# One-stream stages: high and low part of an operand side by side as one moving operand of 512 columns

## The chip, the cores and the metric

The kernel runs on one core of a Trainium2 chip. The metric is the device time of one execution in microseconds, as the median of several runs.

## The reference

Two blocks follow each other on 256 tokens `x` and 256 tokens `ctx` of width 1024, in float32. The first block has two layers, each with an FFN, a mixer (latent attention, a spatial gate and a short convolution) and a second FFN; the second block has two layers, each with a mixer (a scan with gates and a local attention) and an MLP. The modulation of every step comes from `c` and `c_ctx`. In the last layer of each block the context stream ends with the mixer's input, so that from there on only `x` goes on:

```python
def ffn_half_step(h, shift, scale, gate, g, w_in, w_out):
    a, b = jnp.split(modulate(rms_norm(h, g), shift, scale) @ w_in, 2, axis=-1)
    return h + FFN_RESIDUAL_WEIGHT * gate * ((jax.nn.silu(a) * b) @ w_out)

def sq_relu_mlp(h, w1, w2):
    return jnp.square(jax.nn.relu(h @ w1)) @ w2
...
        h = h + mod_l[5] * merge_groups(attn, sg, cv, g_out[l], w_mix_out[l])
        h = ffn_half_step(h, mod_l[6], mod_l[7], mod_l[8], g_ffn2[l], w_ffn2_in[l], w_ffn2_out[l])
        if not last:
            ...
            hc = ffn_half_step(hc, mod_c[6], mod_c[7], mod_c[8], g_ffn2[l], w_ffn2_in[l], w_ffn2_out[l])
```

The FFN is 2816 wide (its first matrix has two halves `a` and `b` of that width), the MLP 4096. The weight matrices are the bulk of the work: every product with one is done to nearly float32 precision, by the splitting told next.

## The kernel before

**Layout.** Features lie on the partitions. The residual stream is eight tiles `h` of 128 x 512 (they print as h_91 to h_98): columns 0 to 255 are `x`, 256 to 511 `ctx`. A two-stream stage works on 512 columns at once, a one-stream stage on the 256 of `x`.

**Splitting.** Every operand of a large product is the sum of a high and a low part in the type fp32r. For weights, `split_weight` has ScalarE copy the raw tile `wr` into `wh` (L316) and VectorE subtract to get `wl` (L317), in pieces of 1024 columns; a weight of 8 x 256 columns is two such pieces, called halves below. For activations, `split_from` does the same with `gh` (L612) and `gl` (L613), and the norm with `xnh` (L615) and `xnl` (L616). The class `Split` holds the parts of an operand, for one stream in two tiles of up to eight k by 256 columns.

**The products.** `mm_feat` computes one output tile of 128 features. For each of the k tiles of the contraction it issues three matmuls into one tile of PSUM: wh by the high part (L346), wh by the low part (L347), wl by the high part (L348), each with its own weight load. A PSUM tile from `psum` is 128 x 512 float32, and five of them (tag "mm") take turns; a one-stream product uses half of one.

**One-stream stages.** They are: the output projection of the last mixer of the first block (operand `ys`), the FFN after it (operands `xn` and `g`; tiles of PSUM `fa` in, `pj` out), the output projection of the last mixer of the second block, and the last MLP. The FFN goes by pairs of tiles: for each tile two products `pa` and `pb`, then `evac`: tanh of `pa` on ScalarE (L751), two VectorE operations with `pa` and `pb` (L752, L753), and the split. Its output is taken in three parts, `part_out`, the MLP's in four. In the output projections `add_residual` takes a finished tile: one VectorE operation h = h + gate x pj (L717).

**Between stages.** As residual tiles are finished, the next norm's `add` squares them and sums over the tiles (L101 on ScalarE, L103 and L106 on VectorE, tiles `acc` and `sq`). Then TensorE sums over features (`nm<-sumto`, L570), VectorE makes the reciprocal root from `ms` (L582) by a short chain on `rs` and `nt` (L584 to L590), TensorE spreads it over the partitions (L564), and the norm's tiles follow. `busy` (L553) are matmuls by the identity without a use for their result. At the very end `Final.add` scales each finished tile into `fy` (L211), and `turn` transposes it on TensorE (`fT`, L219). Within the one-stream FFN the second ctx is loaded and transposed (`xt`, L1768); at its end two tiles of the next mixer's input for ctx are computed (272 columns, L360 to L362), from which `vn` (L1297) and `gates` (L1298) are taken.

**What sets the order.** A scheduler places the instructions of each engine by its own estimate of their times; weights are loaded by SP in the order of use, with three buffers for raw and three for split weights. Within an engine the instructions then run in the order written.

Of the kernel before, what the change touches and what calls it, by code (L numbers as in the profile page):

```python
# [10 lines left out]
F32R = mybir.dt.float32r  # L11
I32 = mybir.dt.int32
AF = mybir.ActivationFunctionType
ALU = mybir.AluOpType
AX = mybir.AxisListType

P = 128
D = 1024
KT = 8
T = 512  # L20
# [22 lines left out]
class Split:  # L43


    def __init__(self, b, n, name, width=T, per=4, joint=False):
        self.b = b
        self.per = per
        self.n = n
        self.width = width  # L50
        self.name = name
        self.joint = joint
        self.parts = {}

    def part(self, which, k):
        g = k // self.per
        n = min(self.per, self.n - self.per * g)
        if (which, g) not in self.parts:
            if self.joint:
                t = self.b.arena([P, 2, n, self.width], F32R, self.name)  # L60
                self.parts["h", g], self.parts["l", g] = t[:, 0], t[:, 1]
            else:
                self.parts[which, g] = self.b.arena([P, n, self.width], F32R, f"{self.name}{which}")
        return self.parts[which, g][:, k % self.per]
# [3 lines left out]

    def L(self, k, c0, c1):
        return self.part("l", k)[:, c0:c1]  # L70


class Weight:
# [36 lines left out]
class Norm(Sumsq):  # L110


    def __init__(self, b, key, gname, gi, sh_chunk, sc_chunk, streams):
        super().__init__(b, streams)
        self.x = b.split(KT, "xn", streams)
        self.key, self.sh_chunk, self.sc_chunk = key, sh_chunk, sc_chunk
        self.gain = (gname, gi)
        self.gs = None
# [117 lines left out]
class Builder:  # L236
# [99 lines left out]
    def mm_feat(self, ps, w, m0, x, c0, c1, ks, first, last, kw0=0, m=P):  # L336
        nc = self.nc
        ks = list(ks)
        o = ps[:m, : c1 - c0]
        for i, k in enumerate(ks):  # L340
            kw = k - kw0
            st = first and i == 0
            en = last and i == len(ks) - 1
            wh = w.h[:, kw, m0 : m0 + m]
            wl = w.l[:, kw, m0 : m0 + m]
            nc.tensor.matmul(o, wh, x.H(k, c0, c1), start=st, stop=False)  # L346
            nc.tensor.matmul(o, wh, x.L(k, c0, c1), start=False, stop=False)  # L347
            self.last_mm = nc.tensor.matmul(o, wl, x.H(k, c0, c1), start=False, stop=en)  # L348
# [270 lines left out]

        return Norm(self, key, gname, gi, sh_chunk, sc_chunk, streams)  # L620

    def split(self, n, name, streams):

        if len(streams) == 1:
            return Split(self, n, name, width=256, per=8)
        return Split(self, n, name)

    @staticmethod
# [18 lines left out]
    def out_proj_steps(self, src, x, ks, gate, streams, group, nxt=None, late=0, ahead=None):  # L647
# [3 lines left out]
        kt = len(ks)  # L651

        def evac(m, j, ps, c0, c1):
            self.add_residual(ps, m + j, gate, c0, c1)
            if nxt is not None:
                for s in range(c0 // 256, c1 // 256):
                    nxt.add(s, m + j)
# [3 lines left out]
        def block(m):  # L661
            w = ahead.pop(m) if m in ahead else self.weight(src[:, m * P : m * P + 256], kt, 256)
            return w, [0, P], m

        m = 0
        if late and len(streams) > 1 and group == 3:

            first = block(0)
            w, offs, _ = first
# [7 lines left out]
            last = block(6)  # L677
# [7 lines left out]
        if late:  # L685
            blocks = [block(0), block(2)]
            m = 4
            c0, c1 = self.spans(streams, False)[0]
# [21 lines left out]
            m = 2 * at.index(e)  # L710
            ahead[m] = self.weight_ahead(src[:, m * P : m * P + 256], KT, 256)

    def add_residual(self, ps, m, gate, c0, c1):

        for s in range(c0 // 256, c1 // 256):
            e0, e1 = 256 * s, 256 * s + 256
            self.nc.vector.scalar_tensor_tensor(self.h[m][:, e0:e1], ps[:, e0 - c0 : e1 - c0], gate[:, m, s : s + 1],  # L717
                                                self.h[m][:, e0:e1], op0=ALU.mult, op1=ALU.add)


    def ffn(self, l, which, streams, x, nxt, side=None, start=None):
        nc = self.nc
        self.one_stream = len(streams) == 1
        key = (0, l)
        a = self.a
# [16 lines left out]
        g = [self.split(t1 - t0, "g", streams) for t0, t1 in parts]  # L742
# [4 lines left out]
        def evac(t, pa, pb, c0, c1):  # L747
            w = c1 - c0
            i = min(t // 8, 2)
            th = self.tmp(T, "th")[:, :w]  # L750
            nc.scalar.activation(th, pa[:, :w], AF.Tanh, scale=0.5)  # L751
            nc.vector.scalar_tensor_tensor(th, th, 1.0, pa[:, :w], op0=ALU.add, op1=ALU.mult)  # L752
            nc.vector.tensor_tensor(th, th, pb[:, :w], op=ALU.mult)  # L753
            self.split_from(th, g[i], t - parts[i][0], c0, c1)
# [1151 lines left out]
```

## Time and profile before

| | us |
|---|---|
| median of 3 runs (lowest, highest) | 2932.84 (2930.45, 2934.3) |
| profiled execution, own time | 2930.02 |
| its span | 2928.3 |
| TensorE busy | 2862.4 |
| VectorE busy | 2127.0 |
| ScalarE busy | 1092.9 |

The mean granted clock of TensorE over the span is 0.991. The span is cut into 40 slices of 73 us on the page; the engines' busy tenths and the clock's:

```profile
PE   8999999999999999999989999999999999999998
PEld 6788899688888888888978999887888889896998
DVE  7888758869887698786796675438698875538665
...
PEclk9999999999999999999999999999999999999999
```

The one-stream stages lie at about 1550 to 1783 us (the first block's last mixer projection and FFN) and 2702 to 2928 us (the second block's last mixer projection and MLP).

### The profile page before, as it was taken

The numbers are of one execution on the slowest core, as the hardware profiler recorded it, in microseconds if no ns is written. First come the engines' busy times: TensorE is split into PE (matmuls) and PEld (weight loads), VectorE is DVE, ScalarE is ACT, GpSimd is POOL, SyncE is SP. The second block draws the span as 40 slices with busy tenths as digits, with TensorE's granted clock in tenths as the row PEclk, the third lists the DMA queues.
The fourth block names the chain that finished last, engine by engine and source line by source line (L and its number), as shares of the span: only waits on it lengthen the run. The fifth ranks groups of instructions, "written<-read, shape, count | busy, mean of one in ns | idle before, by whom it ended". The sixth has DMA issues, their size and how long they took to land.

```text
span 2928.3 us, 44583 instructions
## 1 busy us (share of the span) xinstructions
PE 2862.4 (98%) x17874; PEld 2475.7 (85%) x17874; DVE 2127.0 (73%) x4329; ACT 1092.9 (37%) x2002; POOL 48.1 (2%) x83
## 2 busy tenths in 40 slices
PE   8999999999999999999989999999999999999998
PEld 6788899688888888888978999887888889896998
DVE  7888758869887698786796675438698875538665
ACT  3223235643222233222554444245442223435543
POOL 0000000000000000000000000011000000001000
PEclk9999999999999999999999999999999999999999
DMA  7655523214655346464332554201246551322553
GB/s 247 202 191 193 174 82 113 62 56 155 208 185 189 130 144 201 164 201 159 93 124 81 181 179 149 77 12 55 87 150 204 194 176 61 110 69 82 168 186 109
DMA packets 357612, 410.27 MB, mean 140 GB/s; under 512 B 24067, under 2 KB 297885, under 8 KB 357405
## 3 DMA queue, kind: packets, MB, share of 16 engines
q1 hardware_dynamic: 353512, 403.63, 42.2%
q10 hardware_dynamic: 3892, 3.78, 0.4%
q8 instruction: 141, 2.31, 0.3%
q14 instruction: 67, 0.54, 0.1%
HBM read 406.34 MB, written 1.05 MB: 139 GB/s over the span
## 4 chain that ended last, share of the span: by engine, by line
PE 91%; DVE 5%; ACT 2%; DMA 1%; issue 1%; SPq 0%; POOL 0%; ACTq 0%; DVEq 0%; POOLq 0%
PE pj L346 14%; PE pj L347 14%; PE pj L348 14%; PE fa L346 10%; PE fa L347 10%; PE fa L348 9%; PE pf L346 2%; PE pf L348 2%; PE pf L347 2%; DVE wl L317 1%; PE pj L360 1%; PE pj L361 1%; PE pj L362 1%; PE po L878 1%; PE sc L846 1%; PE ada L511 1%
## 5 line engine op out<-in xcount | busy, mean ns | idle before, releaser
L316 ACT ACTIVATE wh<-wr 128x1024 fp32r<-128x1024 f32 (+3 forms) x542 | 525.7, 1017 | 853.2 <-PE pj L347 437.6
L317 DVE TENSOR_TENSOR wl<-wr,wh 128x1024 fp32r<-128x1024 f32 (+3 forms) x542 | 624.6, 1176 | 180.2 <-ACT wh L316 172.2
L500 DVE SCALAR_TENSOR_TENSOR ad<-wr,silu,ad 128x512 f32<-128x512 f32 x784 | 548.2, 745 | 17.6 <-DMA wr<-in_w_ada_dram 17.6
L347 PE MATMUL fa<-xnl,wh 128*128 128x512 f32 (+1 forms) x1472 | 524.1, 357 | 2.7 <-DVE xnl L616 2.7
L346 PE MATMUL fa<-xnh,wh 128*128 128x512 f32 (+1 forms) x1472 | 521.8, 360 | 3.7 <-ACT xnh L615 3.0
L348 PE MATMUL fa<-xnh,wl 128*128 128x512 f32 (+1 forms) x1472 | 524.1, 357 | 1.1 <-DVE wl L317 1.1
L346 PE MATMUL pj<-gh,wh 128*128 128x256 f32 (+1 forms) x1372 | 457.0, 334 | 0.0
L348 PE MATMUL pj<-gh,wl 128*128 128x256 f32 (+1 forms) x1372 | 455.6, 332 | 0.0
L347 PE MATMUL pj<-gl,wh 128*128 128x256 f32 (+1 forms) x1372 | 455.5, 332 | 0.0
L346 PEld LDWEIGHTS fa<-xnh,wh 128*128 128x128 f32 x1472 | 276.4, 189 | 48.7 <-ACT xnh L615 3.8
L348 PEld LDWEIGHTS fa<-xnh,wl 128*128 128x128 f32 x1472 | 278.5, 189 | 44.8 <-DVE wl L317 1.5
L347 PEld LDWEIGHTS fa<-xnl,wh 128*128 128x128 f32 x1472 | 278.4, 189 | 44.6 <-DVE xnl L616 3.3
L346 PEld LDWEIGHTS pj<-gh,wh 128*128 128x128 f32 x1372 | 258.5, 189 | 28.3 <-ACT wh L316 1.4
L348 PEld LDWEIGHTS pj<-gh,wl 128*128 128x128 f32 x1372 | 258.4, 188 | 27.1
L347 PEld LDWEIGHTS pj<-gl,wh 128*128 128x128 f32 x1372 | 258.6, 189 | 26.2 <-issue 0.2
L347 PE MATMUL pj<-xnl,wh 128*128 128x256 f32 (+1 forms) x824 | 258.4, 319 | 0.1
L348 PE MATMUL pj<-xnh,wl 128*128 128x256 f32 (+1 forms) x824 | 258.1, 318 | 0.0
L346 PE MATMUL pj<-xnh,wh 128*128 128x256 f32 (+1 forms) x824 | 255.2, 319 | 0.4 <-ACT xnh L615 0.2
L348 PEld LDWEIGHTS pj<-xnh,wl 128*128 128x128 f32 x824 | 154.5, 188 | 11.9
L347 PEld LDWEIGHTS pj<-xnl,wh 128*128 128x128 f32 x824 | 154.0, 188 | 11.8 <-issue 0.4
L346 PEld LDWEIGHTS pj<-xnh,wh 128*128 128x128 f32 x824 | 152.2, 188 | 12.8 <-ACT xnh L615 0.8
L717 DVE SCALAR_TENSOR_TENSOR h<-pj,mod,h 128x256 f32<-128x256 f32 x144 | 66.5, 480 | 103.0 <-PE pj L348 102.5
(375 smaller groups left out, 4245.0 us busy)
## 6 DMA issues: line engine op xcount, KB each, us to landing
wr<-in_w_ada_dram SPq DMA_DIRECT2D x112, 1024.0 KB, 5.7
wr<-in_w_ffn_in_dram SPq DMA_DIRECT2D x88, 1024.0 KB, 5.5
wr<-in_w_mlp_dram SPq DMA_DIRECT2D x64, 1024.0 KB, 5.5
wr<-in_w_ffn_out_dram SPq DMA_DIRECT2D x32, 1024.0 KB, 5.1
wr<-in_w_in_dram SPq DMA_DIRECT2D x20, 1024.0 KB, 5.2
wr<-in_w_ffn_out_dram SPq DMA_DIRECT2D x16, 768.0 KB, 5.5
wr<-in_w_mix_in_dram SPq DMA_DIRECT2D x12, 1024.0 KB, 5.3
ar<-in_w_ada_dram SPq DMA_DIRECT2D x8, 1024.0 KB, 12.2
```

The lines of the kernel that those rows point to most:

```text
L316: self.nc.scalar.activation(h[:, i0:i1], raw[:, i0:i1], AF.Copy)
L317: self.nc.vector.tensor_tensor(l[:, i0:i1], raw[:, i0:i1], h[:, i0:i1].bitcast(F32), op=ALU.subtract)
L346: nc.tensor.matmul(o, wh, x.H(k, c0, c1), start=st, stop=False)
L347: nc.tensor.matmul(o, wh, x.L(k, c0, c1), start=False, stop=False)
L348: self.last_mm = nc.tensor.matmul(o, wl, x.H(k, c0, c1), start=False, stop=en)
L360: nc.tensor.matmul(ps_ap, xh, w.h[:, kw, n0:n1], start=st, stop=False)
L361: nc.tensor.matmul(ps_ap, xh, w.l[:, kw, n0:n1], start=False, stop=False)
L362: nc.tensor.matmul(ps_ap, xl, w.h[:, kw, n0:n1], start=False, stop=en)
L500: nc.vector.scalar_tensor_tensor(acc[:, j], raw[:, k - k0], s[:, k, j : j + 1], acc[:, j], op0=ALU.mult, op1=ALU.add)
L511: nc.tensor.matmul(ps[q : q + 32, :P], self.sumto[:, 3 - r : 35 - r], accs[r // 2][:, j, o : o + P], start=(r == 0), stop=(r == 3), tile_p ...
L717: self.nc.vector.scalar_tensor_tensor(self.h[m][:, e0:e1], ps[:, e0 - c0 : e1 - c0], gate[:, m, s : s + 1], self.h[m][:, e0:e1], op0=ALU.m ...
L846: nc.tensor.matmul(ps[:, :w], q_ap(q0), k_ap(k0 * P, (k0 + nk) * P), start=True, stop=bias is None)
```

## The change

For one stream, the parts of an operand lie side by side: `Split` takes tiles of up to four k by 2 by 256 columns, and `both(k)` is the 512 columns of high and low part together. For such an operand `mm_feat` issues two matmuls for each k: wl by the high part into the lower 256 columns of the PSUM tile, and wh by both parts into all 512. In a finished tile, the lower half holds wh by high and wl by high, the upper half wh by low, and their sum is the product. The FFN's `evac` makes it by `whole`: a ScalarE copy of the upper half and a VectorE add of the lower. `add_residual` adds the two halves to `h` one after the other, each times the gate. Of the norms only the one of the first block's FFN is wide; the last MLP's first product stays as it was, while its `g` and both `ys` are wide.

```diff
+        self.wide = wide
...
-            if self.joint:
+            if self.wide:
+                t = self.parts["w", g] = self.b.arena([P, n, 2, self.width], F32R, self.name)
+                self.parts["h", g], self.parts["l", g] = t[:, :, 0], t[:, :, 1]
...
+    def both(self, k):
+        return self.part("w", k).rearrange("p a c -> p (a c)")
...
-        self.x = b.split(KT, "xn", streams)
+
+        self.x = b.split(KT, "xn", streams, key[0] == 0)
...
+        if x.wide:
+
+            for i, k in enumerate(ks):
+                kw = k - kw0
+                wh = w.h[:, kw, m0 : m0 + m]
+                wl = w.l[:, kw, m0 : m0 + m]
+                st = first and i == 0
+                en = last and i == len(ks) - 1
+                turns = [(ps[:m, : c1 - c0], wl, x.H(k, c0, c1), False), (ps[:m, :T], wh, x.both(k), True)]
+                for o, lhs, rhs, wide in turns[::-1] if st else turns:
+                    self.last_mm = nc.tensor.matmul(o, lhs, rhs, start=st and wide, stop=en and wide)
+            return
...
-    def split(self, n, name, streams):
+    def split(self, n, name, streams, wide=True):
...
         if len(streams) == 1:
-            return Split(self, n, name, width=256, per=8)
+            return Split(self, n, name, width=256, wide=True) if wide else Split(self, n, name, width=256, per=8)
         return Split(self, n, name)
...
-            self.add_residual(ps, m + j, gate, c0, c1)
+            self.add_residual(ps, m + j, gate, c0, c1, x.wide)
...
+    def whole(self, x, ps, w):
+
+        if not x.wide:
+            return ps[:, :w]
+        t = self.tmp(w, "wd")
+        self.nc.scalar.activation(t, ps[:, w : 2 * w], AF.Copy)
+        self.nc.vector.tensor_tensor(t, t, ps[:, :w], op=ALU.add)
+        return t
+
+    def add_residual(self, ps, m, gate, c0, c1, wide=False):
+
+        if wide:
+            for i in range(2):
+                self.nc.vector.scalar_tensor_tensor(self.h[m][:, c0:c1], ps[:, 256 * i : 256 * i + 256], gate[:, m, 0:1],
+                                                    self.h[m][:, c0:c1], op0=ALU.mult, op1=ALU.add)
+            return
...
+            pa, pb = self.whole(x, pa, w), self.whole(x, pb, w)
```

In the orders below, a row is line, operation, out<-in with the numbers of the buffers, and the shape. New line numbers stand for old ones: L747 for L717 (residual add), L326 for L317 (weight half), L111 and L114 for L103 and L106 (sum and square), L603 for L582, L1334 for L1298, L220 for L211.

VectorE at the end of the first block's last mixer, from the last tile's residual add to the norm's `ms`. Before:

```order
L717 SCALAR_TENSOR_TENSOR h_98<-pj_13787,mod_6272,h_98 128x256
L103 TENSOR_TENSOR acc_13635<-acc_13635,sq_13748 128x256
L106 TENSOR_TENSOR sq_13785<-h_97 128x256
L317 TENSOR_TENSOR wl_14027<-wr_14024,wh_14026 128x1024
L106 TENSOR_TENSOR sq_13813<-h_98 128x256
L317 TENSOR_TENSOR wl_14027<-wr_14024,wh_14026 128x1024
L582 TENSOR_SCALAR ms_13837<-nm_13821 128x2
```

After:

```order
L747 SCALAR_TENSOR_TENSOR h_98<-pj_13738,mod_6272,h_98 128x256
L326 TENSOR_TENSOR wl_13950<-wr_13947,wh_13949 128x1024
L747 SCALAR_TENSOR_TENSOR h_97<-pj_13717,mod_6272,h_97 128x256
L326 TENSOR_TENSOR wl_13950<-wr_13947,wh_13949 128x1024
L111 TENSOR_TENSOR acc_13616<-acc_13616,sq_13654 128x256
L747 SCALAR_TENSOR_TENSOR h_98<-pj_13738,mod_6272,h_98 128x256
L111 TENSOR_TENSOR acc_13616<-acc_13616,sq_13684 128x256
L111 TENSOR_TENSOR acc_13616<-acc_13616,sq_13706 128x256
L114 TENSOR_TENSOR sq_13736<-h_97 128x256
L114 TENSOR_TENSOR sq_13757<-h_98 128x256
L603 TENSOR_SCALAR ms_13781<-nm_13765 128x2
```

The second adds of h_97 and h_98 stand behind weight halves, and three sums and two squares now follow behind them, ahead of `ms`.

VectorE at the end of that FFN, where the norm of the next mixer starts and the gates of two ctx tiles are taken. Before:

```order
L717 SCALAR_TENSOR_TENSOR h_98<-pj_16099,gate_14538,h_98 128x256
L106 TENSOR_TENSOR sq_16119<-h_98 128x256
L317 TENSOR_TENSOR wl_16325<-wr_16322,wh_16324 128x1024
L1298 TENSOR_TENSOR gates_16193<-pj_16212,bg_16194 128x32
L582 TENSOR_SCALAR ms_16126<-nm_16121 128x2
L584 TENSOR_SCALAR rs_16128<-ms_16126 128x2
L589 SCALAR_TENSOR_TENSOR nt_16130<-rs_16128,ms_16126 128x1 x2
L590 SCALAR_TENSOR_TENSOR rs_16128<-nt_16130,rs_16128 128x2
L1298 TENSOR_TENSOR gates_16193<-pj_16239,bg_16194 128x32
L139 SCALAR_TENSOR_TENSOR nt_16142<-h_91,gs_15373,nm_16121 128x256
```

After:

```order
L747 SCALAR_TENSOR_TENSOR h_97<-pj_15658,gate_14381,h_97 128x256
L747 SCALAR_TENSOR_TENSOR h_98<-pj_15676,gate_14381,h_98 128x256
L111 TENSOR_TENSOR acc_15542<-acc_15542,sq_15629 128x256
L1334 TENSOR_TENSOR gates_15765<-pj_15784,bg_15766 128x32
L111 TENSOR_TENSOR acc_15542<-acc_15542,sq_15647 128x256
L111 TENSOR_TENSOR acc_15542<-acc_15542,sq_15673 128x256
L114 TENSOR_TENSOR sq_15691<-h_98 128x256
L1334 TENSOR_TENSOR gates_15765<-pj_15811,bg_15766 128x32
L603 TENSOR_SCALAR ms_15698<-nm_15693 128x2
L605 TENSOR_SCALAR rs_15700<-ms_15698 128x2
L610 SCALAR_TENSOR_TENSOR nt_15702<-rs_15700,ms_15698 128x1 x2
```

The `gates` of the second ctx tile has moved from behind the chain of `rs` to ahead of `ms`.

VectorE in the last MLP, where the first tile of its last output part is scaled into `fy` for the transpose. Before:

```order
L717 SCALAR_TENSOR_TENSOR h_91<-pj_26676,mod_19868,h_91 128x256
L717 SCALAR_TENSOR_TENSOR h_92<-pj_26708,mod_19868,h_92 128x256
L211 TENSOR_SCALAR fy_26706<-h_91,cols 128x256
L717 SCALAR_TENSOR_TENSOR h_93<-pj_26747,mod_19868,h_93 128x256
L211 TENSOR_SCALAR fy_26737<-h_92,cols 128x256
L317 TENSOR_TENSOR wl_26902<-wr_26899,wh_26901 128x1024
L211 TENSOR_SCALAR fy_26781<-h_93,cols 128x256
L317 TENSOR_TENSOR wl_26902<-wr_26899,wh_26901 128x1024
```

After:

```order
L747 SCALAR_TENSOR_TENSOR h_91<-pj_26024,mod_19440,h_91 128x256
L747 SCALAR_TENSOR_TENSOR h_92<-pj_26049,mod_19440,h_92 128x256
L747 SCALAR_TENSOR_TENSOR h_93<-pj_26081,mod_19440,h_93 128x256
L747 SCALAR_TENSOR_TENSOR h_91<-pj_26024,mod_19440,h_91 128x256
L747 SCALAR_TENSOR_TENSOR h_92<-pj_26049,mod_19440,h_92 128x256
L326 TENSOR_TENSOR wl_26208<-wr_26205,wh_26207 128x1024
L747 SCALAR_TENSOR_TENSOR h_93<-pj_26081,mod_19440,h_93 128x256
L220 TENSOR_SCALAR fy_26047<-h_91,cols 128x256
L220 TENSOR_SCALAR fy_26071<-h_92,cols 128x256
L326 TENSOR_TENSOR wl_26208<-wr_26205,wh_26207 128x1024
```

The first `fy` stood behind two residual adds; it now stands behind six and a weight half.

## Rows read from the trace of the kernel before

**Rows 1.** The page: busy time by engine, and the chain of waits by engine.

```profile
PE 2862.4 (98%) x17874; PEld 2475.7 (85%) x17874; DVE 2127.0 (73%) x4329; ACT 1092.9 (37%) x2002; POOL 48.1 (2%) x83
...
PE 91%; DVE 5%; ACT 2%; DMA 1%; issue 1%; SPq 0%; POOL 0%; ACTq 0%; DVEq 0%; POOLq 0%
```

**Rows 2.** Windows: stretch and length in us, busy PE, PEld, DVE, ACT, POOL, clock, DMA share, GB/s.

```profile
2750.00:2890.00 140.00, 140.00 (x1188) 140.00 (x1187) 88.03 (x128) 68.13 (x102) 0.00 (x0) 1.00 0.61 192
...
1130.00:1188.00 58.00, 58.00 (x254) 47.33 (x253) 44.02 (x65) 14.65 (x18) 0.00 (x0) 1.00 0.60 199
...
2580.00:2590.00 10.00, 10.00 (x81) 10.00 (x80) 2.28 (x3) 2.79 (x6) 0.00 (x0) 1.00 0.33 105
```

**Rows 3.** Lines by form, VectorE, 1600 to 1780: operation, names, shapes, count, busy us, mean ns, idle.

```profile
L317 DVE TENSOR_TENSOR wl<-wr,wh 128x1024 fp32r<-128x1024 f32 x54 | 64.5, 1222 | 26.5 <-ACT wh L316 25.4
L717 DVE SCALAR_TENSOR_TENSOR h<-pj,gate,h 128x256 f32<-128x256 f32 x22 | 10.4, 481 | 11.5 <-PE pj L348 11.4
...
L753 DVE TENSOR_TENSOR th<-th,fa 128x256 f32<-128x256 f32 x22 | 9.2, 418 | 13.6 <-PE fa L348 13.4
```

**Rows 4.** The same view of ScalarE.

```profile
L316 ACT ACTIVATE wh<-wr 128x1024 fp32r<-128x1024 f32 x54 | 54.2, 1051 | 43.1 <-PE pj L347 16.3 <-PE fa L347 16.1 <-issue 6.2
L612 ACT ACTIVATE gh<-th 128x256 fp32r<-128x256 f32 x22 | 9.1, 414 | 30.4 <-DVE th L753 30.4
```

**Rows 5.** Timeline, end of the first block's last mixer: start, length, engine, line, operation, tiles, idle.

```profile
1582.05 1.28 PE L553 MATMUL busy<-ident 128*128 128x128 f32 x10
1582.13 2.00 ACT L316 ACTIVATE wh<-wr 128x1024 fp32r<-128x1024 f32 x2 [1.48 <-PE pj L347]
1582.25 0.48 DVE L717 SCALAR_TENSOR_TENSOR h<-pj,mod,h 128x256 f32<-128x256 f32 x1 [0.24 <-PE pj L348]
...
1584.45 0.42 DVE L106 TENSOR_TENSOR sq<-h 128x256 f32<-128x256 f32 x1
...
1585.92 0.15 DVE L582 TENSOR_SCALAR ms<-nm 128x2 f32<-128x2 f32 x1
```

**Rows 6.** Timeline, start of the one-stream FFN.

```profile
1590.41 0.86 PE L346 MATMUL fa<-xnh,wh 128*128 128x256 f32 x5
1590.52 0.87 DVE L616 SCALAR_TENSOR_TENSOR xnl<-nt,mod,xnh 128x256 fp32r<-128x256 f32 x2
```

**Rows 7.** Timeline, the load of ctx within that FFN.

```profile
1718.57 0.44 PE L1768 MATMUL xt<-ident,tok 128*128 128x128 f32 x2 [1.02 <-DVE th L753]
```

**Rows 8.** Timeline, end of that FFN.

```profile
1783.12 0.29 PE L360 MATMUL pj<-wh,xnh 128*128 128x272 f32 x1
...
1787.29 0.15 DVE L582 TENSOR_SCALAR ms<-nm 128x2 f32<-128x2 f32 x1
...
1790.04 0.61 PE L564 MATMUL nm<-ident,rs 128*128 128x128 f32 x4
...
1791.82 0.39 PE L360 MATMUL pj<-wh,xnh 128*128 128x272 f32 x1 [1.17 <-ACT xnh L615]
```

**Rows 9.** Timeline, end of the second block's last mixer.

```profile
2727.59 1.27 PE L553 MATMUL busy<-ident 128*128 128x128 f32 x10
...
2731.04 0.15 DVE L582 TENSOR_SCALAR ms<-nm 128x2 f32<-128x2 f32 x1
```

**Rows 10.** Timeline, last MLP, start of the last quarter of its output.

```profile
2902.29 0.28 PE L348 MATMUL pj<-gh,wl 128*128 128x256 f32 x1
2902.57 0.35 DVE L211 TENSOR_SCALAR fy<-h,cols 128x256 f32<-128x256 f32 x1
...
2902.97 0.44 PE L219 MATMUL fT<-ident,fy 128*128 128x128 f32 x2 [0.40 <-DVE fy L211]
```

**Rows 11.** Windows, late part of the first block's last mixer projection.

```profile
1560.00:1565.00 5.00, 2.48 (x14) 2.08 (x13) 3.99 (x17) 1.20 (x3) 0.00 (x0) 0.77 0.00 0
...
1565.00:1570.00 5.00, 5.00 (x27) 5.00 (x27) 0.76 (x3) 0.42 (x1) 0.00 (x0) 0.54 0.00 0
...
1570.00:1575.00 5.00, 5.00 (x44) 5.00 (x44) 4.16 (x7) 4.26 (x7) 0.00 (x0) 1.00 0.01 2
```

More of the change, by code (lines that the diff above doesn't have):

```diff
@@ L43, with __init__ @@
 class Split:
-    def __init__(self, b, n, name, width=T, per=4, joint=False):
+    def __init__(self, b, n, name, width=T, per=4, joint=False, wide=False):
         self.b = b
@@ L58, in part @@
         if (which, g) not in self.parts:
-            if self.joint:
+            if self.wide:
+                t = self.parts["w", g] = self.b.arena([P, n, 2, self.width], F32R, self.name)
+                self.parts["h", g], self.parts["l", g] = t[:, :, 0], t[:, :, 1]
+            elif self.joint:
                 t = self.b.arena([P, 2, n, self.width], F32R, self.name)
@@ L711, in prefetch @@
             ahead[m] = self.weight_ahead(src[:, m * P : m * P + 256], KT, 256)
-    def add_residual(self, ps, m, gate, c0, c1):
+    def whole(self, x, ps, w):
[11 more added lines that the diff above has]
+            return
         for s in range(c0 // 256, c1 // 256):
```

## The prediction

> **What bounds the kernel now.** I read the page first. TensorE is busy 98% of the span, and the chain that ended last lies on it for 91% [rows 1]: time is won where TensorE runs dense, and lost where it stops. So I looked next at the rate of its matmuls in dense stretches, by the windows view. In the last one-stream MLP, 1187 weight loads pass in 140 us, one matmul of 256 columns every 117.9 ns, with TensorE and its weight path both busy in all of it. In a two-stream stretch, matmuls of 512 columns follow each other every 229.2 ns (58/253) [rows 2]. The wide one is a little under twice the narrow one: the gain is there, and small. Then I read the timeline at each place where a one-stream stage ends and TensorE waits for the last residual add, because there the change adds work to VectorE that no matmul covers.
>
> **What the change removes.** For one (tile, k) it puts a matmul of 256 and one of 512 columns in the place of three of 256; the columns streamed stay 768. By the rates it saves 2 x 117.9 - 229.2 = 6.6 ns. It applies to 912 such groups: 64 in each of the two last mixer projections, 44 x 8 = 352 into the FFN, 22 x 8 = 176 out of it, 32 x 8 = 256 out of the last MLP. 912 x 6.6 ns = -6.0 us. The trace has no long run in which the two widths alternate, so bounds: if all 768 columns went at the 512 rate, 354 - 344 = 10 ns a group, -9.0 us; if each change of width cost the saving again, 0; nothing excludes a small loss beyond. I take -6.0, the nearest rows.
>
> The Trainium skill ("TensorE: Matmul & The Clock Gate", section "Back-to-back issue gap") gives 131 ns for a sustained matmul of 512 columns. By that a group would go from 354 to 249 ns and the whole change would bring an estimated 96 us; [rows 2] show 229 ns, so I hold to the rows.
>
> **What it adds beside other work.** FFN in-projection: four ScalarE copies and four VectorE adds per pair of tiles. A pair is 32 groups, 11.2 us of TensorE. VectorE does there four weight halves (1.22 us each) and, for two tiles, three operations of about 0.42: 7.4 us, and with four adds of about 0.42 it is 9.1. ScalarE: four halves of 1.05 and two operations of about 0.41 for each of two tiles: 5.8, with four copies 7.4 [rows 3, 4]. Both stay under 11.2, so TensorE hides them. In the out-projections each tile gets a second residual add, 0.48 us; 72 of them, and beside a tile's eight groups (2.8 us) it is hidden too. Were the cover gone, those 72 would be 35 us, which I don't expect. SP's order of the weight loads is the same in both kernels and DMA is busy 0.61 of the time there [rows 2], so no load should come late. What isn't covered is what follows the last tiles.
>
> **What it adds where TensorE waits.** Seven places, each counted from the last matmul E before the wait. A VectorE step takes about 0.42, a weight half 1.2.
>
> 1. End of the last mixer of the first block. Before, E = 1582.05, the add of the last tile runs at once, a square of h follows at 1584.45 to 1584.87, and `ms` of the norm starts 1.05 after it, at 1585.92 = E+3.9 [rows 5]. Afterwards the order has behind the first add of h_98: a weight half, an add, a half, then acc, the second add of h_98, acc, acc, two squares, and only then `ms`. The weight half waits for ScalarE's copy (two halves in 2.00 us from 1582.13 on): E+1.1. Then 2 x 1.2 + 7 x 0.42 = 5.3, the squares end at E+6.4, `ms` at E+7.4: +3.5.
> 2. FFN start. The first wide matmul wants the low part too. Before, TensorE starts at 1590.41 on high parts, and the first two low parts take from 1590.52 to 1591.39 [rows 6]. Now it starts near 1590.95: +0.5.
> 3. The load of ctx within the FFN: TensorE waits behind the last FFN tile's `th` on VectorE and gets its last two transposes off at 1718.57 after 1.02 of idling [rows 7]. One more VectorE step is ahead of it: +0.5 (0 to 1.2).
> 4. FFN end. Beside the norm, TensorE has two tiles of ctx for the next mixer, from E = 1783.12 on; before, the norm's `ms` comes at 1787.29 = E+4.2, the row sums go out at 1790.04, and the next projection starts at 1791.82 = E+8.7 [rows 8]. In the new order `gates` of the second ctx tile stands ahead of `ms`; that tile ends at E + 48 x 0.125 = E+6.0 (80 loads of that width in 10 us [rows 2]), its ScalarE copy and `gates` take it to E+6.8. From `ms` to the row sums the chain needs 2.1 to 2.75, from there to the start 1.8: E+10.8, +2.1.
> 5. End of the last mixer of the second block, the pattern of 1. Before, the wait begins at 2727.59 and `ms` starts at 2731.04 = E+3.5 [rows 9]. Afterwards: a half from E+1.1, two adds, a half, two acc, two squares, 2 x 1.2 + 6 x 0.42 = 4.9, plus 1.05: E+7.1, +3.6.
> 6. Last MLP, start of the last quarter of its output. Before, `fy` of h_91 starts at 2902.57 and the transposes that wait for it at 2902.97, 0.56 after TensorE's last matmul could end (2902.29 + 0.12) [rows 10]. Afterwards the adds of h_91, h_92, h_93 come first, then the second adds of h_91 and h_92, a weight half, the second add of h_93, and then `fy`: 6 x 0.42 + 1.2 + 0.35 less about 0.2 of a head start = 3.8, so +3.2.
> 7. The very last tile has one more add ahead of the output's norm: +0.5.
>
> Sum: 3.5 + 0.5 + 0.5 + 2.1 + 3.6 + 3.2 + 0.5 = +13.9. Each of 1, 5 and 6 could be half as much where a weight copy is ready earlier, so 7 to 15.
>
> **The clock.** From 1560 to 1565 TensorE was busy in 2.48 of 5 us; in the next 5 us the granted clock was 0.54, near the lower level of 1.2 GHz, and 27 loads passed where 44 passed in the 5 us after that [rows 11]: 17/44 x 5 = 1.9 us. Places 1, 4, 5 and 6 get some 3 us more without matmuls (the filler matmuls at 1 and 5 stay as many as they were). One of the four falling costs 2, all of them 8, none 0; I take +2.0. At 1.2 GHz the saving of a group should shrink too, which is too short a time to matter.
>
> **Sum.** -6.0 + 13.9 + 2.0 = +9.9 us on the profiled execution's own 2930.0 (span 2928.3 and 1.7 around it): 2939.9. The median of the runs, 2932.84, stands 2.8 above that execution, so the forecast for the median is 2942.7. Less than 5.9 us (0.2%) from 2932.84 is what I call no change, about what a measurement of this kernel can tell: faster is below 2927.0, slower above 2938.7.
>
> **The rivals.**
> - Half hidden: places 1, 4, 5 and 6 add 1.5 us each for a shorter wait for weights, the others 2.0, the clock doesn't fall: 8.0 - 6.0 = +2, 2934.8, no change. For it: a norm's chain before [rows 5, 9] also had a weight half in it and cost no more than 3.9. Against: the order counts the instructions, and each has a row.
> - Dense after all, the other side: what the wide matmul frees is the weight path, which is busy in all 140 us of the 256-column stretch and in 47.33 of 58 of the 512-column one [rows 2]. If that path, not the columns, sets the 117.9 ns, a group gains up to 10 ns or more: -9.0 us. With stops that cost only their added adds (six of 0.48, the FFN's start hidden: 2.9) the result is -6.1 us, 2926.7; it decides once the stops cost under 3. Against: matmuls of 272 columns, with as many loads, go at 125.0 ns (10/80) [rows 2], by the columns and not by the loads.
> - A faster wide matmul: beside a narrow one it could stream its columns faster than in a run of its own. An eighth less than 229.2 would be 912 x 28.6 ns = -26.1 us on top of -6.0, with +15.9 back -16.2: 2916.6. Against: the 512-column run of [rows 2]. By the figure in the section of the Trainium skill named above it would be more still.
> - The clock falls at all four stops: 8 in place of 2, +15.9, 2948.7. For it: [rows 11]. Against: fillers stand at two of the places.
> - The change not doing what it says: the two halves could not stay in one bank. In the code every such tile of PSUM already is 512 columns wide, so this has no weight.
>
> **Chances.** Forecast 0.58, half hidden 0.24, dense after all 0.08, faster columns 0.02, the clock at all stops 0.08. Of the forecast a twentieth or so ends under 2938.7. So slower 0.63, no change 0.27, faster 0.10. The range takes in the half hidden case's upper half and the clock's: 2931.5 to 2950; the forecast's own is 2938 to 2947.
>
> **What would show it.** In the new profile: alternating starts of 0.118 and 0.229 us in the one-stream stretches, 347 a group; a group at 354 or 340 moves the first term. `ms` behind the last add at E+7.4 and E+7.1 at places 1 and 5; the projection's start at E+10.8 at 4; some 3.8 us of idle ahead of the transposes at 6. A granted clock below 0.8 right behind one of these. What would make it wrong: TensorE idle in the middle of the FFN for lack of a bank or a weight, which I put at nothing, or stops no longer than before.

## The result, and the profile after

The changed kernel takes 2950.83 us (median of 6 runs, 2949.05 to 2959.66) against 2931.64 us for the kernel before (6 runs, 2928.34 to 2934.3): a ratio of 1.0069 with a 95% interval of 1.0057 to 1.0081. It is slower by about 20 us. I had forecast slower, by 10, and a range to 2950.0; the time lies just above it.

The page of the changed kernel, busy time by engine and the chain of waits by engine:

```profile
PE 2866.6 (97%) x16962; PEld 2439.5 (83%) x16962; DVE 2173.7 (74%) x4445; ACT 1107.2 (38%) x2046; POOL 47.6 (2%) x83
...
PE 90%; DVE 6%; ACT 2%; DMA 1%; issue 1%; SPq 0%; POOL 0%; ACTq 0%; DVEq 0%; POOLq 0%
```

TensorE runs 912 matmuls less than in [rows 1] (16962 against 17874), and its busy time has not fallen: 2866.6 us against 2862.4. The share of VectorE on the chain has gone from 5% to 6%: the loss is looked for first where TensorE waits for VectorE.

To see where, I cut the one-stream part of the timeline of each kernel at the first and the last matmul of each stage. Lengths in us, from one profiled execution each (that of the changed kernel is the fastest of its six):

| stretch | before | after | after - before |
|---|---|---|---|
| place 1 and 2: last mixer of the first block, to the FFN's first matmul | 8.20 | 15.34 | +7.1 |
| the FFN, with place 3 | 192.87 | 192.81 | -0.1 |
| place 4: the next mixer's first product, with its start | 37.68 | 41.20 | +3.5 |
| place 5: last mixer of the second block, to the MLP's first matmul | 7.27 | 12.93 | +5.7 |
| the last MLP up to the last part of its output | 158.85 | 159.50 | +0.7 |
| place 6: that last part, to its last matmul | 24.65 | 29.97 | +5.3 |
| place 7: from there to the end of the span | 9.78 | 10.23 | +0.4 |

These are +22.7 together. The spans differ by 19.0 (2947.3 against 2928.3); the rest, -3.7, lies ahead of place 1 (-2.2) and between places 4 and 5 (-1.5), within what such long stretches differ by from one execution to the next (the 880 us between place 4 and the last mixer's output were between 879 and 886 in the profiles of this study).

Place 1 in the timeline of the changed kernel (start, length, engine, line, operation, tiles, count, idle time before):

```profile
1579.86 1.27 PE L574 MATMUL busy<-ident 128*128 128x128 f32 x10
...
1583.56 1.21 DVE L326 TENSOR_TENSOR wl<-wr,wh 128x1024 fp32r<-128x1024 f32 x1
...
1586.28 0.75 DVE L114 TENSOR_TENSOR sq<-h 128x256 f32<-128x256 f32 x2
...
1586.41 1.01 PE L591 MATMUL nm<-sumto,acc 128*128 128x1 f32 x4 [5.29 <-DVE acc L111]
...
1587.29 1.84 PE L591 MATMUL nm<-sumto,sq 128*128 128x1 f32 x8
...
1588.99 3.76 PE L574 MATMUL busy<-ident 128*128 128x128 f32 x16
1589.17 0.16 DVE L603 TENSOR_SCALAR ms<-nm 128x2 f32<-128x2 f32 x1 [2.14 <-PE nm L591]
...
1591.11 0.16 DVE L611 SCALAR_TENSOR_TENSOR rs<-nt,rs 128x2 f32<-128x2 f32 x1
...
1592.55 1.06 PE L585 MATMUL nm<-ident,rs 128*128 128x128 f32 x4
...
1595.36 0.50 PE L358 MATMUL fa<-xn,wh 128*128 128x512 f32 x1 [0.75 <-DVE xn L637]
```

Against [rows 5] the end of the stage, E, is at 1579.86. The weight halves stand ahead of the squares, as in the order, and the squares end at 1587.03 = E+7.2 (before E+2.8). TensorE stands still for 5.29 us. Then the sum of the squares takes 1.84 us and the 16 fillers behind it 3.76; in the kernel before these 16 took 2.64 at place 1 and 2.03 at place 5. `rs` is finished at 1591.27; the matmuls that spread it stand in TensorE's queue behind the fillers and start only at 1592.55, 1.3 later. The FFN starts at E+15.5, before at E+8.4.

Place 5, the same view:

```profile
2734.54 1.28 PE L574 MATMUL busy<-ident 128*128 128x128 f32 x10
...
2741.87 3.76 PE L574 MATMUL busy<-ident 128*128 128x128 f32 x16
2742.04 0.16 DVE L603 TENSOR_SCALAR ms<-nm 128x2 f32<-128x2 f32 x1 [1.53 <-PE nm L591]
...
2743.98 0.16 DVE L611 SCALAR_TENSOR_TENSOR rs<-nt,rs 128x2 f32<-128x2 f32 x1
...
2745.42 1.06 PE L585 MATMUL nm<-ident,rs 128*128 128x128 f32 x4
```

The pattern again: `ms` at 2742.04 = E+7.5 (before E+3.5 [rows 9]), 16 fillers in 3.76 us, `rs` ready at 2744.14 and spread at 2745.42.

Place 4, the same view:

```profile
1788.00 0.29 PE L381 MATMUL pj<-wh,xnh 128*128 128x272 f32 x1
...
1794.40 0.58 PE L591 MATMUL nm<-sumto,sq 128*128 128x1 f32 x4
1794.64 0.19 DVE L1334 TENSOR_TENSOR gates<-pj,bg 128x32 f32<-128x32 f32 x1 [1.10 <-ACT vn L1333]
1795.03 0.16 DVE L603 TENSOR_SCALAR ms<-nm 128x2 f32<-128x2 f32 x1 [0.19 <-PE nm L591]
...
1799.00 0.59 PE L381 MATMUL pj<-wh,xnh 128*128 128x272 f32 x1 [1.11 <-ACT xnh L636]
```

`gates` of the second ctx tile is ahead of `ms`, which comes at E+7.0 (before E+4.2), and the projection starts at 1799.00 = E+11.0 (before E+8.7 [rows 8]). But `gates` is not what `ms` waits for last: it is done at 1794.83, and `ms` waits another 0.19 us for the row sums. On TensorE these stood between the matmuls of the ctx tiles before; now they stand behind the last of them.

Place 6, the same view:

```profile
2915.27 2.05 DVE L747 SCALAR_TENSOR_TENSOR h<-pj,mod,h 128x256 f32<-128x256 f32 x5 [3.31 <-PE pj L358]
...
2917.24 1.22 DVE L326 TENSOR_TENSOR wl<-wr,wh 128x1024 fp32r<-128x1024 f32 x1
...
2918.77 0.61 DVE L220 TENSOR_SCALAR fy<-h,cols 128x256 f32<-128x256 f32 x2
...
2919.17 0.69 PE L228 MATMUL fT<-ident,fy 128*128 128x128 f32 x2 [3.46 <-DVE fy L220]
```

Five residual adds, a weight half, another add, and then `fy`: TensorE idles 3.46 us for it, against 0.40 in [rows 10]. The 16 matmuls of the next tile then take 5.47 us from first to last, those of each later tile 3.05.

The clock right behind these places, by the windows view (columns as in [rows 2]); the second row is from place 3, the load of ctx:

```profile
1585.00:1590.00 5.00, 3.58 (x17) 3.59 (x18) 2.65 (x11) 0.42 (x1) 0.00 (x0) 0.50 0.77 240
...
1723.00:1728.00 5.00, 4.85 (x19) 4.11 (x20) 4.64 (x12) 1.89 (x5) 0.00 (x0) 0.66 0.60 191
1798.00:1803.00 5.00, 4.00 (x22) 4.00 (x23) 5.00 (x13) 2.95 (x7) 0.00 (x0) 0.66 0.00 0
2740.00:2745.00 5.00, 5.00 (x27) 5.00 (x28) 2.36 (x13) 0.00 (x0) 0.00 (x0) 0.56 0.72 215
2917.00:2922.00 5.00, 2.83 (x10) 2.55 (x11) 4.64 (x10) 1.85 (x5) 0.00 (x0) 0.61 0.00 0
```

In each of the four the granted clock fell to between 0.50 and 0.66, so to the lower level for a part or all of the window. It fell at place 3 as well, which I had not counted: from 1718 to 1723 TensorE was busy 3.05 of 5 us with transposes and waits of up to 1.03 us. The kernel before was not free of such a fall either, at place 1, where TensorE stood still for no more than 0.69 us at a time:

```profile
1587.00:1592.00 5.00, 4.96 (x30) 4.66 (x30) 3.58 (x13) 1.49 (x4) 0.00 (x0) 0.70 0.66 211
```

And the dense stretches of the changed kernel, in the same view: the FFN's first product, and an MLP product that is still narrow:

```profile
1597.00:1649.00 52.00, 52.00 (x298) 45.44 (x297) 38.31 (x70) 29.94 (x57) 0.00 (x0) 1.00 0.50 160
2852.00:2872.00 20.00, 20.00 (x169) 20.00 (x168) 13.35 (x21) 11.28 (x21) 0.00 (x0) 1.00 0.51 170
```

By this count a group of a wide and a narrow matmul takes 2 x 52/297 = 350 ns in the FFN. A window also counts the matmuls that its edges cut, so short windows come out too fast; the mean between the starts of neighbours in the timeline is better. By it a group takes 350.4 ns in the FFN's first product, where three narrow matmuls took 353.4: 3 ns saved, not 6.6. In the first piece of the MLP's output it takes 353, where three took 359. The last row holds no wide matmul at all, and yet its narrow ones start 120.0 ns apart (20/168 = 119.0 by the count), where they were 117.8 apart.

### The profile page after: what moved, and what is told of

It is laid out like the page before. It is cut to its first block, busy times and chain, and to the rows that moved or that the text cites. A ratio compares the mean times of both kernels' runs of the same rounds, so it can differ in the third digit from the quotient of the medians.

```text
span 2947.3 us, 42928 instructions
## 1 busy us (share of the span) xinstructions
PE 2866.6 (97%) x16962; PEld 2439.5 (83%) x16962; DVE 2173.7 (74%) x4445; ACT 1107.2 (38%) x2046; POOL 47.6 (2%) x83
## 4 chain that ended last, share of the span: by engine, by line
PE 90%; DVE 6%; ACT 2%; DMA 1%; issue 1%; SPq 0%; POOL 0%; ACTq 0%; DVEq 0%; POOLq 0%
PE pj L367 11%; PE pj L369 11%; PE pj L368 11%; PE fa L367 8%; PE fa L368 8%; PE fa L369 8%; PE pj L358 6%; PE fa L358 4%; PE pf L367 2%; PE pf L369 2%; PE pf L368 2%; DVE wl L326 2%; PE pj L381 1%; PE pj L382 1%; PE pj L383 1%; PE sc L882 1%
## 5 line engine op out<-in xcount | busy, mean ns | idle before, releaser
L326 DVE TENSOR_TENSOR wl<-wr,wh 128x1024 fp32r<-128x1024 f32 (+3 forms) x542 | 624.2, 1174 | 158.3 <-ACT wh L325 148.4
L368 PE MATMUL fa<-xnl,wh 128*128 128x512 f32 (+1 forms) x1120 | 424.1, 380 | 2.7 <-DVE xnl L637 2.7
L367 PE MATMUL fa<-xnh,wh 128*128 128x512 f32 (+1 forms) x1120 | 423.1, 384 | 2.9 <-ACT xnh L636 2.3
L369 PE MATMUL fa<-xnh,wl 128*128 128x512 f32 (+1 forms) x1120 | 424.9, 381 | 1.1 <-DVE wl L326 1.1
L367 PE MATMUL pj<-gh,wh 128*128 128x512 f32 (+1 forms) x940 | 335.8, 358 | 0.0
L369 PE MATMUL pj<-gh,wl 128*128 128x512 f32 (+1 forms) x940 | 334.0, 356 | 0.0
L368 PE MATMUL pj<-gl,wh 128*128 128x512 f32 (+1 forms) x940 | 333.1, 354 | 0.0
L367 PEld LDWEIGHTS pj<-gh,wh 128*128 128x128 f32 x940 | 177.1, 188 | 27.5 <-ACT wh L325 1.2
L369 PEld LDWEIGHTS pj<-gh,wl 128*128 128x128 f32 x940 | 176.5, 188 | 27.2
L368 PEld LDWEIGHTS pj<-gl,wh 128*128 128x128 f32 x940 | 177.0, 188 | 25.8 <-issue 0.2
L358 PE MATMUL pj<-g,wh 128*128 128x512 f32 x432 | 152.6, 403 | 0.0
```

Of the source, the lines that this page charges most:

```text
L326: self.nc.vector.tensor_tensor(l[:, i0:i1], raw[:, i0:i1], h[:, i0:i1].bitcast(F32), op=ALU.subtract)
L358: self.last_mm = nc.tensor.matmul(o, lhs, rhs, start=st and wide, stop=en and wide)
```

## The experiments

All ratios are to the kernel before on the same chip, with 95% intervals; the lengths of stretches are from one profiled execution of each kernel. The theory: the loss is made by the second residual add behind the last tiles, by the weight halves that the order then puts ahead of the norm, and by the clock that falls in the longer stops. The rival: it is made in the dense stretches, by the wide matmul or the layout.

**The layout alone.** Parts side by side, but narrow matmuls and one add:

```diff
-        if x.wide:                       # mm_feat
+        if False:
...
-            self.add_residual(ps, m + j, gate, c0, c1, x.wide)
+            self.add_residual(ps, m + j, gate, c0, c1)
...
-        if not x.wide:                   # whole
+        if True:
```

> The parts lie side by side as in the changed kernel, but the products are three narrow matmuls and one residual add again. Theory A (the cost is the second residual adds behind the last tiles, and the clock that falls in the longer stops): 2930 to 2934, no more than 0.1% from before, with the stops of before. Rival B (the cost sits in the dense stretches, in how the operands now lie): 2937 or more.

Measured: 1.0006 (0.9997 to 1.0015). The four stops are as before (8.21, 37.60, 7.26, 24.71 us for the rows of places 1 and 2, 4, 5 and 6), so the layout does not make the loss. But it isn't free. Two dense stretches of it, by windows:

```profile
1600.00:1640.00 40.00, 40.00 (x339) 40.00 (x338) 24.28 (x36) 19.74 (x30) 0.00 (x0) 1.00 0.49 158
2845.00:2855.00 10.00, 10.00 (x85) 10.00 (x85) 5.41 (x10) 6.09 (x10) 0.00 (x0) 1.00 0.63 210
```

and the same of the kernel before:

```profile
1600.00:1640.00 40.00, 40.00 (x342) 40.00 (x341) 27.11 (x41) 21.35 (x32) 0.00 (x0) 1.00 0.53 176
2845.00:2855.00 10.00, 10.00 (x87) 10.00 (x86) 6.82 (x12) 5.53 (x12) 0.00 (x0) 1.00 0.50 160
```

341 against 338 loads in the same 40 us. Between neighbouring matmuls the mean is 117.8 ns before in the FFN and in most pieces of the MLP (119.8 in the first piece of its output); here it is 118.9 in the FFN and 120.0 in the MLP's first product, whose operand the change doesn't even touch. The FFN is 1.4 us longer than before and the MLP 1.7.

**Two adds, narrow.** The layout alone, and a second add of each one-stream tile with a factor of zero:

```diff
-                self.nc.vector.scalar_tensor_tensor(..., ps[:, 256 * i : 256 * i + 256], gate[:, m, 0:1],
+                self.nc.vector.scalar_tensor_tensor(..., ps[:, 0:256], self.sumto[:, 0:1] if i else gate[:, m, 0:1],
```

> Narrow matmuls, parts side by side, but each residual add of a one-stream tile is followed by a second one of the same size, of the product times zero, so that the result doesn't change. Theory A: as slow as the changed kernel or a little slower, since the gain is missing: 2948 to 2954, with some 5 us without matmuls at the end of each block's last mixer and the clock near 0.5 behind them. Rival B (the wide matmul or the layout costs it): at most 2938.

Measured: 1.0088 (1.0073 to 1.0104), 2954.7 us. Without one wide matmul the kernel is as slow as the changed one, or slower, and its four stretches are 13.92, 41.30, 11.41 and 28.54 us long: 17.4 us more than before, where the changed kernel has 21.6 more. Another 3 us are the layout's, in the dense stretches. The window behind its first stop:

```profile
1585.00:1590.00 5.00, 2.48 (x12) 2.51 (x12) 3.04 (x7) 0.00 (x0) 0.00 (x0) 0.57 0.74 245
1590.00:1595.00 5.00, 5.00 (x24) 5.00 (x25) 2.14 (x12) 0.00 (x0) 0.00 (x0) 0.50 0.22 76
```

The second add with the order that follows from it makes most of the loss; the rival falls.

**Wide in the FFN's first product alone.**

```diff
-    def split(self, n, name, streams, wide=True):
+    def split(self, n, name, streams, wide=False):
```

> The wide matmul in the FFN's first product alone; the operands of all output projections are as before, with one residual add. Theory A: 2930 to 2934 (352 groups at 2.7 ns are -1.0 us, the start of the FFN +0.5, the load of ctx +0.5). Rival B: a third or more of the loss stays, 2937 or more.

Measured: 0.9998 (0.9990 to 1.0007). No loss, and no gain that can be told. The start of the FFN (place 2) is 0.6 later than before (8.84 against 8.20), as the term for it said.

**Longer fillers.** Behind both mixers:

```diff
-    BUSY = (5, 8, 4)
+    BUSY = (20, 8, 4)
```

> The changed kernel with 40 filler matmuls in the place of 10 behind each block's last mixer, some 5 us at full clock, so that TensorE does not stand still while VectorE finishes. If the clock is a part of the loss: the row sums and the second fillers run at full clock, each of the two stops is 1.5 to 2.5 us shorter, 2945.5 to 2948. If VectorE's adds alone make the stop: 2949.5 to 2952.

Measured: 1.0057 (1.0043 to 1.0071), 2945.76 us, 3.5 us less than the changed kernel by the ratios, whose intervals overlap; so the stops themselves have to show it. Place 1 in its timeline:

```profile
1580.31 4.62 PE L574 MATMUL busy<-ident 128*128 128x128 f32 x40
...
1588.23 2.03 PE L574 MATMUL busy<-ident 128*128 128x128 f32 x16
1588.41 0.16 DVE L603 TENSOR_SCALAR ms<-nm 128x2 f32<-128x2 f32 x1 [0.92 <-PE nm L591]
...
1590.36 0.16 DVE L611 SCALAR_TENSOR_TENSOR rs<-nt,rs 128x2 f32<-128x2 f32 x1
...
1590.58 0.71 PE L585 MATMUL nm<-ident,rs 128*128 128x128 f32 x4 [0.32 <-DVE rs L611]
...
1593.05 0.50 PE L358 MATMUL fa<-xn,wh 128*128 128x512 f32 x1 [0.86 <-DVE xn L637]
```

Here the clock stays at 1.00. VectorE is no faster: `ms` waits for the same adds and halves. But it starts at E+8.1 and not at E+9.3, 16 fillers take 2.03 us, `rs` is spread the moment it is ready (1590.58), and the FFN starts at E+12.7. The stretch of place 1 and 2 is 12.58 us against 15.34: 2.8 us were the clock's, and what is left, 4.4 above before, is VectorE's. At place 5 the stretch is 11.35 against 12.93, but there the clock still fell behind the row sums, and 16 fillers took 2.83 us:

```profile
2741.00:2746.00 5.00, 4.52 (x31) 4.53 (x32) 2.95 (x14) 0.00 (x0) 0.00 (x0) 0.79 0.72 214
```

So 1.6 us is the least that the clock cost at place 5. At place 3 the clock stayed up in this execution: the first 20 matmuls behind the load of ctx take 3.59 us, in the changed kernel 5.12, and the FFN with them is 191.25 us long, 1.6 less.

**Wide first.** In each tile the wide matmuls of all k, then the narrow ones:

```diff
+            for wide in (True, False):
+                for i, k in enumerate(ks):
...
+                    o, rhs = (ps[:m, :T], x.both(k)) if wide else (ps[:m, : c1 - c0], x.H(k, c0, c1))
```

> The changed kernel, but each tile's wide matmuls of all k come first and its narrow ones after them, so that the width changes twice a tile and not sixteen times. If the change of width is what ate the saving (351 to 353 ns a group measured, 347 by the rates of the kernel before): 347 a group, some 4 us faster than the changed kernel, 0.5% to 0.6% above before. If a wide matmul of this kind is slower wherever it stands: 0.65% to 0.75% above before, as the changed kernel.

Measured: 1.0052 (1.0039 to 1.0065), 2947.32 us. The expected time, but for another reason. In the FFN's first product a group takes 348.9 ns by the starts (230.9 and 118.0), against 350.4 with the widths in turns, and the product's 160 groups take 55.90 us and not 56.10. On 352 groups that is some 0.5 us: the change of width ate little of the saving. Place 4 got 1.2 us longer (42.43). Most of the time came from place 6, 5.8 us, which I had not thought of:

```profile
2919.65 1.00 DVE L747 SCALAR_TENSOR_TENSOR h<-pj,mod,h 128x256 f32<-128x256 f32 x2 [1.53 <-PE pj L358]
...
2920.84 0.48 DVE L747 SCALAR_TENSOR_TENSOR h<-pj,mod,h 128x256 f32<-128x256 f32 x1 [0.19 <-PE pj L358]
...
2921.24 0.34 DVE L220 TENSOR_SCALAR fy<-h,cols 128x256 f32<-128x256 f32 x1
...
2921.83 0.38 PE L228 MATMUL fT<-ident,fy 128*128 128x128 f32 x2
```

A tile's matmuls now end one tile after another, so the scheduler puts `fy` behind three adds and ahead of the weight half, and the last part takes 24.18 us, before 24.65, with the two adds of each tile still there. At place 6 the order, not the second adds by themselves, had made the stop.

**Narrow where a norm follows.** The wide matmuls and the two adds only inside:

```diff
-            self.add_residual(ps, m + j, gate, c0, c1, x.wide)
+            self.add_residual(ps, m + j, gate, c0, c1, x.wide and nxt is None)
...
+            ... self.mm_feat(..., wide=nxt is None)
```

> Wide matmuls only where no norm follows the product: the FFN in, its first two output parts and the first three of the MLP; the products with a norm behind them (both mixers' outputs, the last part of the FFN and of the MLP) are narrow with one residual add, on the same layout. Theory A (the loss is behind the last tiles): no loss, within 0.1% of before, and 0.05% under it if the groups save 2 ns each (672 x 2 = 1.3 us). Rival B (the loss is in the dense stretches): 0.3% or more above before.

Measured: 1.0001 (0.9992 to 1.0009). Within that interval the whole loss is behind the last tiles. A gain can't be told.

**Weight halves behind the squares.** The changed kernel, the last weight's halves queued behind the norm's last square:

```diff
+            b.last_sq = nc.vector.tensor_tensor(sq, ap, ap, op=ALU.mult)
...
+                with self.tc.issue_after(self.last_sq.ins) if len(streams) == 1 and t == 0 and o else nullcontext():
```

> The changed kernel, but the last weight's halves that stood on VectorE ahead of the norm's squares at the end of both mixers are queued behind the squares. If these halves, put there by the new order, make half of the two long stops: each is 2.4 us shorter and its clock stays up, 0.45% to 0.55% above before. If the residual adds alone do it: 0.65% to 0.75%, as the changed kernel.

Measured: 1.0058 (1.0045 to 1.0070): less than I expected, with an interval that reaches both cases. Place 1:

```profile
1583.75 1.27 PE L574 MATMUL busy<-ident 128*128 128x128 f32 x10
...
1586.75 0.42 DVE L114 TENSOR_TENSOR sq<-h 128x256 f32<-128x256 f32 x1
...
1587.09 4.62 DVE L326 TENSOR_TENSOR wl<-wr,wh 128x1024 fp32r<-128x1024 f32 x4
...
1591.63 0.15 DVE L603 TENSOR_SCALAR ms<-nm 128x2 f32<-128x2 f32 x1
```

The last square ends at 1587.17 = E+3.4, 3.8 us earlier than in the changed kernel. But the scheduler puts all four halves, 4.62 us, between it and `ms`, which starts at E+7.9: the wait came back one step later. The two long stops are 2.5 and 2.0 us shorter, but the clock fell in them all the same, and place 4 is 1.5 longer (42.65).

**Upper half first.** Wide first, and the add of the upper half ahead of that of the lower:

```diff
-            for i in range(2):
+            for i in (1, 0):
```

> As the kernel with the wide matmuls first in each tile, and the residual add of the upper half ahead of that of the lower: the upper half is complete while the narrow matmuls still run, so that add can lie beside TensorE and only one is left behind the last matmul. If the second add by itself is the cost: 2 us or more faster than that kernel. If the order of the weight halves is: the same as that kernel within 1 us.

Measured: 1.0056 (1.0044 to 1.0069), the same as wide first. Around the weight halves the adds stand in the same order as before the edit, and the long stops are the same (14.91 and 12.89 us). Which half is added last makes no difference. That the order decides at these two stops fits this, but this run doesn't show it.

**High parts first in the tile.** The layout alone, with the high parts of a tile together:

```diff
-                t = self.parts["w", g] = self.b.arena([P, n, 2, self.width], F32R, self.name)
-                self.parts["h", g], self.parts["l", g] = t[:, :, 0], t[:, :, 1]
+                t = self.b.arena([P, 2, n, self.width], F32R, self.name)
+                self.parts["h", g], self.parts["l", g] = t[:, 0], t[:, 1]
```

> Narrow matmuls and one residual add, as with the layout alone, in the same tiles, but all high parts of a tile first and all low parts behind them, not in turns. With the layout alone, narrow matmuls started every 118.9 ns in the FFN and 120.0 in the last MLP's first product, against 117.8 before. If the alternation of high and low parts slows the reading: 117.8 in the FFN again. If it is where the tiles come to lie in memory: 118.7 to 120 as with the layout alone. The time is within 0.15% of before by both.

Measured: 1.0005 (0.9996 to 1.0015), and 118.9 ns in the FFN, 120.0 in the MLP's first product. It isn't the alternation of parts. Where the tiles come to lie would be another cause, but that was not tried: it stays open what costs 1 to 2 ns a matmul.

**Wide first and longer fillers.**

> Wide matmuls first in each tile, and 40 fillers in the place of 10 behind both mixers. If the two parts of the account are apart from each other (the last MLP's wait for the transpose, gone by the first; the clock in the two long stops, by the second): 3.5 to 4.5 us faster than the first alone, 0.36% to 0.42% above before. If they overlap: 0.5%.

Measured: 1.0036 (1.0022 to 1.0050), 2941.15 us, 4.7 less than with wide first alone by the ratios. Within what these can tell, the two parts add up. In this execution the clock stayed up through place 5:

```profile
2745.00:2750.00 5.00, 3.99 (x34) 3.61 (x33) 3.63 (x16) 0.00 (x0) 0.00 (x0) 1.00 0.74 227
```

Its stretch there is 10.70 us long, 2.2 less than in the changed kernel and in wide first (12.94), and 3.4 above before. Places 1 and 4 still had a fall (13.16 and 42.62 us).

**Inside, wide first.** The two edits above joined:

> The wide matmuls only inside, where no norm follows, and the wide ones first in each tile. By the stages of the two kernels it joins, 672 groups save 3 to 4 ns against the kernel before and no stop is longer: 2 to 2.5 us, 0.07% to 0.09% under before, which would be the fastest version; by rival B, 0.3% above.

Measured: 0.9996 (0.9988 to 1.0005), 2929.14 against 2930.36 us. The FFN is 190.78 us long, 2.1 less than before, but place 2 takes 0.8 of it back and the MLP 0.4. It has the lowest ratio of these versions, and can't be told from the kernel before.

## Why the prediction was wrong

The mechanism and the places were right, and so was the sign; two terms of the sum were mis-sized, both to the same side. By the steps of the prediction:

- *The seven places, +13.9 for VectorE.* Right in sum. With the clock taken out, places 1 and 2 are +4.4 (forecast 4.0) by the run with longer fillers, place 5 +3.4 (3.6) by the run with wide first as well. At place 3 the gap between the last FFN matmul and the next product went from 3.9 to 4.7, +0.8 (0.5). Place 4 restarts at E+11.0 (E+10.8), +2.3 (2.1). Place 6 is +3.1 by its idle time (3.2), place 7 +0.4 (0.5). That is 14.4. The +4.4 is measured from a kernel that had a fall of the clock of its own there, so VectorE's share may be a little more. At place 4 the number is right in part by luck: `ms` waited last for the row sums on TensorE, not for `gates`, and the two were ready within 0.2 us of each other.
- *The clock, "I take +2.0".* This step failed. I priced one fall out of four at 1.9 us, the loads missing in a dense stretch behind it. The clock fell at all four, the rival to which I gave 0.08, and at place 3, which stood in no rival. It cost 2.8 at place 1 by the run with longer fillers, 2.2 at place 5 by that with wide first as well, and 1.6 at place 3 by the former, where the clock did not fall. At place 4 the stretch grew by 1.2 more than its start moved, at place 6 by 2.2 more than its idle time; that these two are the clock is worked out from the windows above, not from a run that takes it away. Together about 10. The fillers, which I had counted against this rival, did not prevent it: the first ten ended long before the stop of 5.3 us did, and the next 16, at half clock, held up the matmuls that spread the norm by 1.3 us at places 1 and 5 each.
- *The saving of 6.6 ns a group, -6.0.* This failed too, though the wide matmul does save that against narrow ones on the same layout. By the mean between neighbours in the FFN's first product, three narrow matmuls take 353.4 ns before, 356.7 with the layout alone, and a wide and a narrow one 350.4 in the changed kernel: 6.3 less than on the same layout, 3.0 less than before. The layout, which I had not priced at all, ate half of it. It also slowed the MLP's first product, which stays narrow, by 1.4 us in its four pieces. Without the gap and the clock of place 3 the FFN is 2.5 us shorter than before, and the wide part of the MLP ahead of place 6 0.8, so that some 1.8 are left and not 6.0. A part of the miss is in the reading: 229.2 ns is a window's count, and the starts of the same stretch are 230.2 apart, which makes 6.0 ns a group of the 6.6.
- *Sum.* 14.4 for VectorE, 10 for the clock and -1.8 saved are +22.6, the table's +22.7 within rounding; I had -6.0 + 13.9 + 2.0 = +9.9. The range, too, was drawn too low for the case that came: the clock's rival at 2948.7 lay at its edge.
- *Small slips that carry nothing.* What the prediction calls the row sums at 1790.04 is the matmul that spreads the norm. Halving places 1, 5 and 6 gives 8.8 as the low end, not 7.
- *No saving at half clock.* Right: behind place 3 a wide and a narrow matmul take 0.64 us together, and three narrow ones behind place 6 of the kernel with two adds take 0.64 too.
- *Cover beside other work.* Right: the copies and adds of the FFN's product cost nothing that shows (56.2 us with them in the kernel with that product alone, 56.9 before).
- *"Half hidden"*, 0.24: wrong. Nothing of the orders' waits was hidden.
- *"Dense after all"*, and a faster wide matmul beside a narrow one: wrong. A wide one next to narrow ones started its successor after 231 to 235 ns in the changed kernel, not under 229. The figure of 131 ns in the Trainium skill ("TensorE: Matmul & The Clock Gate", section "Back-to-back issue gap") does not hold for these matmuls either, by the same starts.

## What to carry to other kernels

An operation added to the evacuation of every tile (its way out of PSUM) cost nothing that shows beside dense matmuls here, and its full price, several times over, behind the last tiles of a stage: count the instructions between the last matmul and the first of the next stage in the new order, and expect the scheduler to put other work between them. Price a longer stop with the clock: behind each of the four stops that grew the rows show a fall to half clock, and behind a load with short waits and one stage of the kernel before they show one too, so count it at every stop. A fixed number of filler matmuls covers a stop of one length; when the stop grows, the fillers behind it run at half clock, ahead of the matmuls that the next stage waits for. And before a saving of 2% per matmul is counted, change the layout alone and look at the rate.

## What the runs showed that I had not expected

The same narrow matmul, on operands of the same shape, started every 117.8, 118.9 or 120.0 ns, steadily through most pieces of a stage. It changed with how the tiles around it were cut, even where its own operand was not touched, and one piece of the kernel before was at 119.8 already; the order of high and low parts within a tile made no difference. And 16 filler matmuls took 3.76 us at half clock where 2.03 were taken at full, in a queue that a norm's result had to pass.
